# Channel shuffle on one core: the small first tiles replaced by full ones

## The chip, the cores and the metric

The kernel runs on one core of one Trainium2 chip. The time is the device time of one execution in microseconds (us); less is better. Engines named here: VectorE (DVE in the profile) copies within the on-chip memory SBUF, SyncE (SP) and ScalarE (ACT) issue transfers here and do nothing else, and 16 DMA engines move the bytes between HBM and SBUF.

## The reference

```
x: (16, 64, 64, 256) float32, groups = 8
x = x.reshape(batch, h, w, groups, 32)
x = x.transpose(0, 1, 2, 4, 3)
out = x.reshape(batch, h, w, 256)
```

Each of the 65,536 pixels has 256 channels, 1 KB. Within a pixel the channels are read as 8 groups of 32 and written as 32 sets of 8: out[j*8 + g] = x[g*32 + j]. No arithmetic is done. The kernel must read 67.1 MB and write 67.1 MB.

## The kernel before

The input is seen as one flat run of pixels. A piece of q slots is 128 x q pixels: partition p of SBUF holds q consecutive pixels, q KB, so each partition row of a transfer is one contiguous run of q KB in HBM and in SBUF. `_SLOTS` says how the 512 slots are cut: a list of tiles, each a list of its pieces. The first tile has two pieces, of 4 and 8 slots; the second has one of 28; then come twelve tiles of 38 and one of 16.

Every tile takes a load buffer and a store buffer of 38 KB a partition (`biggest`), from a pool of two (`_IN_BUFS`) and of three (`_OUT_BUFS`), in turn. The loop over the tiles (line 45) does for each one:

- line 55: SP issues the load of each piece. It must wait until the copy that last read this load buffer, two tiles back, has ended.
- line 57: VectorE copies each piece from the load buffer to the store buffer and permutes the channels on the way. It waits for the piece's load, and for the store that last used this store buffer, three tiles back.
- line 61: ACT issues the store of each piece, after its copy.

The order on each engine is that of the program; nothing else schedules. So there are two DMA queues, SP's for all loads and ACT's for all stores, each in program order, and both run on the same 16 DMA engines. At the start the loads of the first two tiles are issued without a wait; every later load is issued at the end of a copy, together with a store.

Of the kernel before, what the change touches and what calls it, by code (L numbers as in the profile page):

```python
# [1 line left out]

# [4 lines left out]


F32 = mybir.dt.float32
P = 128  # L10

_SLOTS = [[4, 8], [28]] + [[38]] * 12 + [[16]]
_IN_BUFS = 2
_OUT_BUFS = 3


@with_exitstack
def kernel(
    ctx: ExitStack,
    tc: tile.TileContext,  # L20
    x: bass.AP,
    groups: bass.AP,
    out: bass.AP,
):
    nc = tc.nc
    b, h, w, c = x.shape
    G = int(groups)
    CPG = c // G
    assert G * CPG == c
    assert sum(map(sum, _SLOTS)) * P == b * h * w  # L30
    biggest = max(map(sum, _SLOTS))

    x_flat = x.rearrange("b h w c -> (b h w c)")
    out_flat = out.rearrange("b h w c -> (b h w c)")

    in_pool = ctx.enter_context(tc.tile_pool(name="in_pool", bufs=_IN_BUFS))
    out_pool = ctx.enter_context(tc.tile_pool(name="out_pool", bufs=_OUT_BUFS))

    def rows(flat, first, q):

        return flat[first * c : (first + P * q) * c].rearrange("(p f) -> p f", p=P)

    ctx.enter_context(tc.manual_schedule(engines=None))
    first = 0
    for parts in _SLOTS:
        in_tile = in_pool.tile([P, biggest * c], F32, name="in_tile")
        out_tile = out_pool.tile([P, biggest * c], F32, name="out_tile")
        at = 0
        pieces = []
        for q in parts:  # L50
            pieces.append((q, first, slice(at * c, (at + q) * c)))
            first += P * q
            at += q
        for q, start, cols in pieces:
            nc.sync.dma_start(out=in_tile[:, cols], in_=rows(x_flat, start, q))  # L55
        for q, start, cols in pieces:
            nc.vector.tensor_copy(  # L57
                out=out_tile[:, cols].rearrange("p (i j g) -> p i j g", j=CPG, g=G),
                in_=in_tile[:, cols].rearrange("p (i g j) -> p i j g", g=G, j=CPG),
            )  # L60
            nc.scalar.dma_start(
                out=rows(out_flat, start, q), in_=out_tile[:, cols]
            )


# [1 line left out]
_INS = ['x', 'groups']  # L67
_OUTS = [((16, 64, 64, 256), 'float32')]

_NUMBERS = {'groups': 8}  # L70


# [26 lines left out]
```

## Time and profile before

| | before |
|---|---|
| time, median of 3 runs | 316.04 us (316.04 to 316.05) |
| profiled execution, span | 314.4 us |
| time less the span of the profiled execution | 1.6 us |
| VectorE busy | 119.0 us, 16 copies |
| copy of 38 slots | 8.79 us, 12 times |
| copies of 4, 8, 28, 16 slots | 1.09, 2.02, 6.57, 3.87 us |
| bytes moved | 134.22 MB, 427 GB/s over the span |
| first load issued, first copy, first store issued | 0.73, 4.06, 5.19 us |
| last copy starts | 294.54 us |
| issue to landing, load and store of 38 slots (median) | 37.0 and 42.6 us |

The page of the profile shows one execution. Its slices are fortieths of the span, and a digit there is the busy share in tenths; the DMA row is the mean over the 16 DMA engines. Queue q1 holds the loads (SP), q10 the stores (ACT). The chain is the list of steps that ended last, followed back from the last instruction; the view of waits adds up who waited for whom. A window is a stretch of the span with the busy time of each engine and the rate of the transfers in it; DMA packets are counted where they start, so a window of few packets may show a share over 1.

The profiled execution itself is longer than its span by what lies before the first and after the last instruction, which the profile doesn't show; the difference to the median of the timed runs is in the table.

### The profile page before, as it was taken

Reading aid. Unit: us, or ns where it says so; the run is one execution under the profiler, and the core shown is the slowest. Engines: PE = TensorE matmul, PEld = TensorE weight load, DVE = VectorE, ACT = ScalarE, POOL = GpSimd, SP = SyncE. Lnnn points to the kernel's source line nnn. Section 1 sums busy time; section 2 is a strip of 40 time slices with the busy share of each in tenths; the row PEclk is TensorE's granted clock in tenths of the full one; section 3 lists DMA queues with packets and bytes.
Section 4 is the critical chain, followed back from the end, with each engine's and each line's share of the span. In section 5 each row is a group of like instructions: output and inputs, shape, how many; then the busy total and the mean of one; then the engine's idle time right before and its main releaser. Section 6 shows DMA issues by size and latency. Waiting matters only on the chain.

```text
span 314.4 us, 132 instructions
## 1 busy us (share of the span) xinstructions
DVE 119.0 (38%) x16; POOL 0.2 (0%) x4
## 2 busy tenths in 40 slices
DVE  2081907309109109019028028037046055065400
POOL 0000000000000000000000000000000000000000
DMA  7999999999999999999999999999999999999997
GB/s 317 405 441 416 435 416 483 401 465 406 450 421 446 426 436 436 401 470 396 475 396 475 396 470 401 470 401 470 401 450 421 446 426 436 436 417 450 429 421 321
DMA packets 4608, 134.22 MB, mean 427 GB/s; under 512 B 512, under 2 KB 512, under 8 KB 768
## 3 DMA queue, kind: packets, MB, share of 16 engines
q1 hardware_dynamic: 2304, 67.11, 49.8%
q10 hardware_dynamic: 2304, 67.11, 49.4%
HBM read 67.11 MB, written 67.11 MB: 427 GB/s over the span
## 4 chain that ended last, share of the span: by engine, by line
DMA 76%; DVE 19%; issue 0%; SPq 0%; DVEq 0%
DMA in_tile<-in_x_dram 76%; DVE out_tile L57 19%; SPq L55 0%; DVEq L57 0%
## 5 line engine op out<-in xcount | busy, mean ns | idle before, releaser
L57 DVE COPY out_tile<-in_tile 128x9728 f32<-128x9728 f32 (+4 forms) x16 | 119.0, 7440 | 179.4 <-DMA in_tile<-in_x_dram 179.4
L80 POOL MEMSET const-uint8-127<- 128x1 uint8 x1 | 0.1, 103 | 0.0
L80 POOL MEMSET const-bfloat16-1.0<- 128x1 bf16 x1 | 0.1, 102 | 0.0
L80 POOL MEMSET const-float32-1.0<- 128x1 f32 x1 | 0.1, 100 | 0.0
L80 POOL MEMSET const-float32-0.0<- 128x1 f32 x1 | 0.1, 99 | 0.2 <-issue 0.2
## 6 DMA issues: line engine op xcount, KB each, us to landing
in_tile<-in_x_dram SPq DMA_DIRECT2D x12, 4864.0 KB, 37.0
out_dram<-out_tile ACTq DMA_DIRECT2D x12, 4864.0 KB, 42.6
in_tile<-in_x_dram SPq DMA_DIRECT2D x1, 3584.0 KB, 14.7
out_dram<-out_tile ACTq DMA_DIRECT2D x1, 3584.0 KB, 30.9
in_tile<-in_x_dram SPq DMA_DIRECT2D x1, 2048.0 KB, 30.4
out_dram<-out_tile ACTq DMA_DIRECT2D x1, 2048.0 KB, 15.2
in_tile<-in_x_dram SPq DMA_DIRECT2D x1, 1024.0 KB, 5.4
out_dram<-out_tile ACTq DMA_DIRECT2D x1, 1024.0 KB, 25.0
```

Source lines behind the costliest of these rows:

```text
L57: nc.vector.tensor_copy(out=out_tile[:, cols].rearrange("p (i j g) -> p i j g", j=CPG, g=G), in_=in_tile[:, cols].rearrange("p (i g j) -> ...
L80: nc = _bacc.Bacc("TRN2", target_bir_lowering=False, num_devices=1)
```

## The change

The cut of the 512 slots is another one. The tile of 4 and 8 slots and the tile of 28 slots at the head are gone; there are thirteen tiles of 38 slots, and the last tile has 18 slots in place of 16. The buffers (38 KB a partition, two for loads, three for stores), the loop and the engines stay as they are. Of 16 loads, 16 copies and 16 stores, 14 of each remain.

```
-_SLOTS = [[4, 8], [28]] + [[38]] * 12 + [[16]]
+_SLOTS = [[38]] * 13 + [[18]]
 _IN_BUFS = 2
 _OUT_BUFS = 3
```

## The prediction

> **What bounds the kernel now.** I read the page first: busy time, the 40 slices, the queues and the chain.
>
> ```profile
> span 314.4 us, 132 instructions
> ...
> DVE 119.0 (38%) x16; POOL 0.2 (0%) x4
> ...
> DMA  7999999999999999999999999999999999999997
> ...
> q1 hardware_dynamic: 2304, 67.11, 49.8%
> q10 hardware_dynamic: 2304, 67.11, 49.4%
> ...
> DMA 76%; DVE 19%; issue 0%; SPq 0%; DVEq 0%
> ```
>
> The 16 DMA engines are busy for 49.8 + 49.4 = 99.2% of the span; every slice but the first and last shows 9. VectorE works 38%. The chain gives 19% to the copies, but a chain passes through whatever released the next step. While VectorE copies, the other queue and the next load keep the DMA engines running, so only a copy during which both queues are empty would cost time. The view of waits agrees: all of VectorE's waiting is for loads, none for a free store buffer.
>
> ```profile
> DVE out_tile L57 <- DMA in_tile<-in_x_dram: 179.4, 16, 14.3
> ```
>
> Then the windows (the head, from copy to copy, the end) show how fast the bytes move in each stage (columns: window, its length, VectorE busy, GpSimd busy, clock, DMA share, GB/s).
>
> ```profile
> 1.50:2.00 0.50, 0.00 (x0) 0.00 (x0) 1.00 0.74 90
> 2.00:2.50 0.50, 0.00 (x0) 0.00 (x0) 1.00 0.45 164
> 2.50:3.00 0.50, 0.00 (x0) 0.00 (x0) 1.00 1.02 418
> 71.31:278.19 206.88, 79.13 (x9) 0.00 (x0) 1.00 1.00 433
> 294.54:313.30 18.76, 3.87 (x1) 0.00 (x0) 1.00 0.95 410
> 313.30:314.40 1.10, 0.00 (x0) 0.00 (x0) 1.00 0.00 0
> ```
>
> From 71.31 to 278.19 lie nine periods, each one 4,980,736-byte load and one such store: 9 x 9.961 MB in 206.88 us is 433.4 GB/s, 22.99 us a period. All 134.22 MB at that rate take 309.7 us. The span has 4.7 us more: 1.75 us before the first bytes (nothing moves before 1.5; the first row is a ramp), 1.1 us after the last ones, and some 1.9 us of small losses in between. So nothing big is to be had from the order of work; the question is whether the change opens a hole in which the DMA engines are empty.
>
> Last, the DMA view in windows that hold one size of row. A transfer is 128 partition rows, 8 on each engine (the page's 4608 packets are 32 transfers of 128 rows and 16 end marks).
>
> ```profile
> DMA packets 80, 1.31 MB, mean 437 GB/s; under 512 B 0, under 2 KB 0, under 8 KB 0
> ...
> q10 hardware_dynamic: 80, 1.31, 101.8%
> ```
>
> ```profile
> DMA packets 88, 3.42 MB, mean 428 GB/s; under 512 B 0, under 2 KB 0, under 8 KB 0
> ...
> q10 hardware_dynamic: 88, 3.42, 98.9%
> ```
>
> The first is 309 to 312 us, 16 KB rows of the last store: 3 us x 16 x 1.018 / 80 = 0.611 us a row. The second is 298 to 306 us, 38 KB rows: 8 x 16 x 0.989 / 88 = 1.438 us. The line through both is 0.009 + 0.0376 us per KB; it gives 0.160 for 4 KB, 0.310 for 8, 1.062 for 28, 0.686 for 18. Loads fit it: 2.6 to 3.4 us (4 KB, 80 rows, 100.1%) gives 0.160, and 4 to 5.5 us (8 KB, 77 rows, 102.1%) gives 0.318, 2% above it.
>
> **The change, part by part.**
>
> *Rows and instructions.* Work per engine before: 2 x 8 x (0.160 + 0.310 + 1.062 + 0.611) = 34.3 us for the four odd sizes, and 24 x 8 x 1.438 = 276.1 for the 38 KB ones, 310.4 in all. After: 26 x 8 x 1.438 = 299.1, and 2 x 8 x 0.686 = 11.0, 310.1. **Saved: 0.3 us**, all of it fixed cost of rows that are no longer there. SP and ACT issue 14 DMAs each where they issued 16 (0.33 and 0.36 us each), and VectorE makes 13 copies of 8.79 and one of 18 slots: (8.791 - 3.873) / 22 = 0.2235 us a slot, so 3.873 + 2 x 0.2235 = 4.32; in sum 118.6 for 119.0. These lie under the DMA engines' work and count nothing.
>
> *The head.* Now only loads move until the first store at 5.19; after the change nothing but loads moves until the first 38 KB tile is copied. Step by step: issue at 0.73, first bytes 1.75, the ramp costs 0.45 (90 and 164 GB/s against 433 in the rows above, beyond the 1.75), then 8 x 1.438 = 11.5: the load ends at 13.7. Its copy starts 0.6 later (the 4 KB load now: 1.75 + 0.45 + 8 x 0.160 = 3.48, copy at 4.06), at 14.3, and ends at 23.1. Here ACT issues the first store and SP the third load, as the third load waits for that copy to free the first of the two load buffers. From an issue to its first bytes it took 1.02 us (0.73 to 1.75), so both queues have work at 24.1. The second load covers all this: it was issued right behind the first, and its rows last until 13.7 + 11.5 = 25.2. **The cover is 1.1 us; no hole, and the later first store costs nothing**, as a byte that is loaded early is a byte that need not be loaded later. That head has some 15 rows of loads alone on each engine, 21.6 us. By the rows above loads alone run between the line and 2% over it: 0 to 0.43 us, of which I take half, **0.2 us paid**.
>
> [...]
>
> *What goes with the old head.* The window from 30.18 to 71.31 us (copies 4 to 6, with 28 KB stores still draining) moves 17.50 MB in 41.13 us, which at 433.4 GB/s would take 40.38: 0.75 us are lost, and from 32 to 36 us the rate is 397 GB/s. Rows are counted where they start, and half a 38 KB row per engine is 0.7 us, so the true loss is between nothing and 0.75; I take the middle, 0.37, and that it doesn't come again, since after the change all rows there are alike. **0.37 us regained**; its bounds are 0 and 0.75.
>
> *The middle.* Both queues hold 38 KB rows, half the rate each, period 22.99 as now. A copy needs the store three tiles back: the fourth copy, about 72, needs the first store, which runs from 24 to 48. No wait is added on VectorE.
>
> *The tail.* At 24 us, 15 of 112 load rows per engine are done. The 89 left of 38 KB alternate with stores: 89 x 2 x 1.438 = 256, to 280; the 8 of 18 KB with 8 stores: 8 x (0.686 + 1.438) = 17, to 297. Left are 7 store rows of 38 KB (10.1 us, to 307.3) and 8 of 18 KB (5.5). The last copy must be stored before 307.3: its load lands by 299 (loads under store traffic reached VectorE about 2 us late), copy 4.3, issue 1.0: 304.4. Cover 2.9. The store before it is needed at 295 (seven pairs of 2.12 after 280) and there by 282 + 8.8 + 1.0 = 292. Cover 3. Now the last copy ends at 298.4 and the stores at 313.3, so neither tail shows.
>
> *Sum.* -0.3 + 0.2 - 0.37 = -0.46 us on a span of 314.4, to 313.9. The median stands 1.6 us over the span (316.04), and that part stays: **315.6 us**. With the terms at their bounds: from -0.3 - 0.75 = -1.05 to -0.3 + 0.43 = +0.13, 315.0 to 316.2.
>
> **The rivals.**
>
> *A hole at 25 us: slower.* Place: between the end of the second load's rows and the first bytes of the third load or first store. Against it: 1.02 us from issue to bytes at the start. For it: the store issued at 5.19 had no row under way by 9.0 (the window 4 to 9 us holds rows of the load queue alone), 3.8 us or more. There, though, load rows stood ahead, and nothing ran empty. Price: an issue that takes x us leaves x - 2.1 empty. It counts as slower when the hole eats the 0.46 and 0.63 more, at x = 3.2; at 3.9 the hole is 1.8 and the time 316.04 - 0.46 + 1.8 = 317.4. Chance 0.11.
>
> *Loads alone are slower than the mix.* For: 410 GB/s from 2.6 to 3.4, with loads only; against: 4 KB rows explain it, and the stores alone keep 1.438. If 410 held for 38 KB rows, 21.6 us become 22.8: 316.04 - 0.3 + 1.2 = 316.9, slower. Chance 0.08. [...]
>
> *The whole small loss was the mixed sizes' own.* Then the sum is at its low end, 315.0.
>
> **How the numbers follow.** A measurement of this kernel can tell about 0.2%, 0.63 us, from no change: under 315.41 is faster, over 316.67 slower. Engines full throughout: 0.76; of its range 315.0 to 316.2 about two fifths lie under 315.41: 0.30 faster, 0.46 the same. The hole: 0.08 slower, 0.03 too small to tell. Loads alone slower: 0.06 and 0.02. What I don't see: 0.05, slower. The range is 315.0 to 316.7: the first case, and the small ends of the others.
>
> **What would show it.** Right: first copy near 14.3, first store and third load issued near 23.1, DMA share 9 in the slices around 25 us, periods of 22.99, no wait of VectorE for a store, and last bytes near 312.8. Wrong: a dip in a window of 24 to 28 us (the hole), under 425 GB/s from 3 to 23 us (loads alone), or longer periods. The last could come from loads and stores that now change over within a row or two of each other, where they were several us apart; the change between two stores alone, near 308, shows no dip in the slices, so I put nothing there.

## The result, and the profile after

| | before | after |
|---|---|---|
| time, median of 4 runs each | 316.05 us | 332.5 us (332.08 to 332.61) |
| ratio | | 1.0515, 95% interval 1.0502 to 1.0528 |
| span of the profiled execution | 314.4 us | 330.8 us |
| VectorE busy | 119.0 us | 118.7 us |

The kernel is 5% slower, 16.4 us; 315.6 was forecast. The page of the kernel after shows nothing of it at first sight:

```profile
span 330.8 us, 121 instructions
...
DVE 118.7 (36%) x14; POOL 0.2 (0%) x4
...
DMA  8999999999999999999999999999999999999994
...
q10 hardware_dynamic: 2016, 67.11, 50.5%
q1 hardware_dynamic: 2016, 67.11, 47.7%
```

The DMA engines are as busy as before (98.2% for 99.2%), VectorE still waits for loads alone, and its waits are longer, 198.6 us in all for 179.4:

```profile
DVE out_tile L57 <- DMA in_tile<-in_x_dram: 198.6, 14, 17.6
```

So the engines are not idle; the same bytes keep them busy for longer. One thing stands out: the two queues moved the same bytes, but the stores (q10) took 50.5% of a longer span and the loads 47.7%, where they were nearly equal (49.4 and 49.8%). The DMA view of the window from 100 to 200 us, in the middle of the steady part, makes it a time per row (a line of a queue has its packets, MB, and the time of its packets as a share of 16 engines' window):

```profile
DMA packets 1191, 41.21 MB, mean 412 GB/s; under 512 B 132, under 2 KB 132, under 8 KB 132
...
q10 hardware_dynamic: 596, 20.62, 52.4%
q1 hardware_dynamic: 595, 20.58, 47.6%
```

The same window of the kernel before:

```profile
DMA packets 1247, 43.54 MB, mean 435 GB/s; under 512 B 128, under 2 KB 128, under 8 KB 128
...
q10 hardware_dynamic: 624, 21.79, 50.4%
q1 hardware_dynamic: 623, 21.75, 50.3%
```

16 engines have 1600 us in the window. After: 20.62 MB are 530 store rows of 38,912 bytes, 1600 x 0.524 / 530 = 1.582 us each, and the loads 1600 x 0.476 / 529 = 1.440. Before both are 1.440. So **a store row takes 10% longer, a load row not**. The windows put the rest of the loss in its place:

```profile
24.00:26.00 2.00, 0.00 (x0) 0.00 (x0) 1.00 1.24 389
26.00:28.00 2.00, 1.30 (x1) 0.00 (x0) 1.00 0.81 195
28.00:30.00 2.00, 2.00 (x1) 0.00 (x0) 1.00 0.96 389
30.00:32.00 2.00, 2.00 (x1) 0.00 (x0) 1.00 0.81 350
71.00:296.00 225.00, 79.10 (x9) 0.00 (x0) 1.00 1.00 412
```

From 24 to 32 us 331 GB/s on average, 1.9 us behind 433. From 71 to 296 us it is 412 GB/s for 433. The third and the thirteenth copy in the timeline:

```profile
53.00 8.97 DVE L57 COPY out_tile<-in_tile 128x9728 f32<-128x9728 f32 x1 [17.55 <-DMA in_tile<-in_x_dram]
296.08 8.77 DVE L57 COPY out_tile<-in_tile 128x9728 f32<-128x9728 f32 x1 [15.29 <-DMA in_tile<-in_x_dram]
```

These are 10 periods of 24.31 us for the 22.99 of before, 13.2 us lost. The store rows themselves are 8 x 0.142 = 1.14 us a period, 11.4 in ten. Most of the rest is in the first two periods, 24.68 and 25.09 us, in which the slowest engine falls behind the others; the eight after them average 24.16. The dip and the ten periods make 15.1 of the 16.4 us. The saving of 0.3 us has to be made good too; what is left, 1.6 us, is the ramp at the start, the stores that are slow before 53 us, and the engines' uneven end (197 GB/s from 323 to 330 us), less what the old head lost.

What sets the slow rows apart is seen in the trace's single DMA records. They don't name the engine, but a row starts within some 4 ns of the end of the one before it on its engine, so the rows can be put into 16 chains. In these, while both queues have work, load and store rows take strict turns on each engine (595 packets of loads and 596 of stores from 100 to 200 us); a turn is one row of 38 KB here, 1.44 us of a load and 1.58 of a store. A transfer is 8 rows and an end mark on each engine, nine turns, in both queues (2016 packets a queue are 14 transfers x 16 engines x 9), so the distance between them, once set, stays, as the table below shows. In the kernel after the end marks of a load and a store come on the same engine in the same moment, and store row r runs directly behind load row r. In the kernel before store row 0 runs behind load row 2. Start of the end marks in us, kernel after, from the records (first, median and last engine of each transfer):

```
third to sixth load    48.2  51.1  52.6 |  71.2  75.1  77.2 |  94.2  99.3 102.3 | 117.1 123.5 126.7
first to fourth store  50.6  51.1  52.6 |  74.1  75.1  77.2 |  97.0  99.3 102.3 | 120.1 123.5 126.7
```

Median and last are the same in both rows: 15 engines, more or less, in step. The first engine isn't: its stores end some 2.9 us, one row of each kind, behind its loads, its store rows take 1.44 us, and this engine alone keeps 23.0 us a period (48.2, 71.2, 94.2, 117.1). At 187.8 us it has run so far ahead that no row of the next load, issued at 184.2, has come. Load and store start together there, and from then on it takes 24 to 25 us like the others (end marks 211.8, 236.5, 260.6).

### The profile page after: what moved, and what is told of

The parts are those of the page before. It is cut to its first block, busy times and chain, and to the rows that moved or that the text cites. A ratio compares the mean times of both kernels' runs of the same rounds, so it can differ in the third digit from the quotient of the medians.

```text
span 330.8 us, 121 instructions
## 1 busy us (share of the span) xinstructions
DVE 118.7 (36%) x14; POOL 0.2 (0%) x4
## 2 busy tenths in 40 slices
DMA packets 4032, 134.22 MB, mean 406 GB/s; under 512 B 448, under 2 KB 448, under 8 KB 448
## 3 DMA queue, kind: packets, MB, share of 16 engines
q10 hardware_dynamic: 2016, 67.11, 50.5%
q1 hardware_dynamic: 2016, 67.11, 47.7%
## 4 chain that ended last, share of the span: by engine, by line
DMA 78%; DVE 17%; issue 0%; SPq 0%; DVEq 0%
DMA in_tile<-in_x_dram 78%; DVE out_tile L57 17%; SPq L55 0%; DVEq L57 0%
## 5 line engine op out<-in xcount | busy, mean ns | idle before, releaser
L57 DVE COPY out_tile<-in_tile 128x9728 f32<-128x9728 f32 (+1 forms) x14 | 118.7, 8477 | 198.6 <-DMA in_tile<-in_x_dram 198.6
```

The costliest lines, as they stand in the source:

```text
L57: nc.vector.tensor_copy(out=out_tile[:, cols].rearrange("p (i j g) -> p i j g", j=CPG, g=G), in_=in_tile[:, cols].rearrange("p (i g j) -> ...
```

## The experiments

**Turns.** Four theories: (1) a store row is slow when the row just before it on its engine is the load of the same number, into the same partition; (2) it is the coinciding end of two transfers; (3) the distance of the two rows in HBM; (4) all engines storing at once. The tool is a small extra load of 16 x n partitions into a scratch tile, which nobody reads: on one queue it takes n rows and an end mark on each engine, n + 1 turns (with 16 partitions the page of `first30_s2` below counts 16 rows and 16 end marks more than that of `first30`, 4064 packets for 4032). The ratios below are to the kernel before, with their 95% intervals.

`s_later2`: the kernel after, with

```
             nc.scalar.dma_start(out=rows(out_flat, start, q), in_=out_tile[:, cols])
+            if first == 38 * P:
+                nc.scalar.dma_start(out=turn_tile[:16, :], in_=...)   # 16 rows of x
```

> The kernel after, with one 8 KB load of 16 partitions put on ACT's queue behind the first store: one row and one end mark for each DMA engine, so from there on each store row comes two turns later against the loads. Theory 1 (same partition): a store row is slow, 1.58 us for 1.44, when the row the engine moved just before it was the load into the same SBUF partition; two turns later it never is. Period back from 24.16 to 22.99 us, 11.6 us less of slow rows and some 2.5 less of uneven engines at the end: 318.5 us, 317.5 to 319.5. Theory 2 (load and store transfers change over at the same moment) and theory 3 (the two rows lie at a fixed distance in HBM) expect the same here. Theory 4 (all engines storing at the same moment are limited by the write side) expects no change: 332.5.

320.1 us (1.0127, 1.007 to 1.0183). The DMA view from 100 to 200 us:

```profile
q10 hardware_dynamic: 627, 21.64, 50.1%
q1 hardware_dynamic: 615, 21.44, 49.7%
```

1600 x 0.501 / 556 = 1.442 us a store row, and two extra turns in one place have taken 12.4 us off; the time is 0.6 us above the expected range. Theory 4 falls, since all engines still store at once. What is left, 4 us over the kernel before, is the hole at 25 us (78 GB/s from 26 to 28 us, 370 in the next two), the first store, which is slow until the shift takes hold, and an uneven end: 37 GB/s from 316 to 318 us.

`before_l3` and `before_l2`: the kernel before, the same load on SP's queue (32 and 16 partitions). It stands behind the load of the first 38-slot tile, at 8.9 us in the timeline; the expectations call that tile the second.

```
             nc.sync.dma_start(out=in_tile[:, cols], in_=rows(x_flat, start, q))
+            if first == 78 * P:
+                nc.sync.dma_start(out=turn_tile[:32, :], in_=...)     # before_l2: [:16]
```

> The kernel before, with one 16 KB load of 32 partitions put on SP's queue behind the load of the second 38-slot tile: two rows and one end mark for each engine, so the loads come three turns later against the stores. In the kernel before a store row follows the load row of three partitions further on; three turns later it follows the load into its own partition. Theories 1, 2 and 3: the stores turn slow, 1.58 us a row, periods of about 24.1 us, some 10 periods: 316.0 + 10 x 1.15 + 2 = 328 to 331 us. Theory 4: 316.1.

316.5 us (1.0008, 0.9997 to 1.0019): no change, and store rows of 1600 x 0.497 / 552 = 1.441 us. The same view, 100 to 200 us:

```profile
q1 hardware_dynamic: 624, 21.79, 50.4%
q10 hardware_dynamic: 616, 21.48, 49.7%
```

I had counted one turn too many: in the kernel before it is load row 2 that store row 0 runs behind, and the records give a row's place in its transfer, not its partition. In those of `before_l3` store row 0 runs directly *ahead* of load row 0, and the end marks of both queues coincide. So the miss is of use: theory 2 falls, since the ends coincide and nothing is slow.

> The kernel before, with one 8 KB load of 16 partitions on SP's queue behind the load of the second 38-slot tile: loads come two turns later, so store row r runs directly behind load row r on each engine, as in the kernel after. (In the kernel before store row 0 follows load row 2; with three turns it came just ahead of load row 0, and nothing was slow.) Theory 1 (a store row directly behind the load row of the same number, which lies in the same partition): stores turn slow from about 50 us on, 10 periods of 24.1 us for 23.0, 326 to 331 us. Were the slow stores of the kernel after due to its head (uneven engines, late first store): 316.3.

327.1 us (1.0348, 1.0318 to 1.0378). The same view, 100 to 200 us:

```profile
q10 hardware_dynamic: 600, 20.86, 53.1%
q1 hardware_dynamic: 592, 20.55, 47.5%
```

1600 x 0.531 / 536 = 1.585 us a store row, the loads 1.439. With its head, its sizes and its even engines untouched, the kernel before becomes slow by an 8 KB load that sets the turns as in the kernel after. That it is not the extra load as such, `before_l3` shows, which has a larger one.

The order doesn't act at once, though. In the records of the kernel after, rows 0 to 3 of the first store (28.0 to 39.3 us) run directly behind the load rows of the same number on 15 engines and take 1.44 us; rows 4 to 7 take 1.48, 1.54, 1.57 and 1.62. In `before_l2_half` below, the rows in this order take 1.44 us up to 60 us, and 1.69 on average from 64 to 80. On the other side, of the 38 KB store rows that run behind a load row of another number in the kernel before, `before_l3`, `s_later2` and `first12_s4`, over 5,500 in all, none takes over 1.5 us. So the order is needed, but it isn't the whole condition: something builds up first, and no run here shows what.

`read_next_row` and `read_mirrored`: the kernel after, reading elsewhere

```
+            off = 38 if q == 38 else 0                           # read_next_row
+            in_=rows(x_flat, start + off, q)
+            src = 12 * 38 * P - start if q == 38 else start      # read_mirrored
+            in_=rows(x_flat, src, q)
```

> The kernel after, but each 38-slot load reads HBM 38 pixels a partition further on (what the neighbour partition should get), so the output is shifted: the distance in HBM between a load row and the store row behind it changes by 38 KB, to that which the one fast engine has, while SBUF partitions, turns and queues stay. Theory 3 (distance in HBM): stores fast, 318.5 us. Theories 1, 2 and 4: 332 us, store rows 1.58 us.

> The kernel after, but the thirteen 38-slot loads read HBM in the reverse order of tiles (the output has the tiles in the wrong places): the distance in HBM between a load row and the store row behind it is another for every tile. Theory 1: as slow as the kernel after, every store row some 1.58 us, 330 to 333 us. Theory 3 (distance in HBM): most tiles fast, under 322 us, and rows that differ from tile to tile.

331.2 and 330.5 us, store rows 1.588 and 1.573, from the stores' lines of the two views of 100 to 200 us (528 and 543 rows):

```profile
q10 hardware_dynamic: 592, 20.55, 52.4%
q10 hardware_dynamic: 609, 21.13, 53.4%
```

At a distance of 38 KB more, and at another one for every tile, the rows are as slow: theory 3 falls as far as these distances go, all of them multiples of 38 KB. That the one fast engine has the first of these distances was my estimate, from its stores lying one row behind; the records have no addresses.

`pad`: `in_pool.tile([P, biggest * c + 176], F32, ...)` in the kernel after.

> The kernel after with 704 B of padding behind each load buffer, so that load and store buffers lie at another distance within a partition; turns, partitions and HBM as in the kernel after. Theory 1 in its plain form (same partition, whatever the address in it): 331 to 333 us, store rows 1.58 us. If it is the address within the partition that collides: 317 to 320.

329.6 us, store rows 1.556, which neither forecast had: with the buffers moved by 704 B within the partition the rows are 0.03 us shorter and the time 3 us, but it isn't cured. `warm` below is 3 us shorter as well, with the buffers where they were, so the 3 us can't be put down to the address.

**One engine or all.** `before_l2_one` and `before_l2_half`: `before_l2` with `turn_tile[:1, :]` and `turn_tile[:8, :]`.

> The kernel before, with a load of one partition (512 B) on SP's queue behind the load of the second 38-slot tile: it goes to one DMA engine alone, so that only this engine's loads come two turns later and its store row r falls directly behind load row r. Theory 1 in the form that the order on an engine itself makes its store rows slow: one engine at 24.1 us a period, the others at 22.99, and the one sets the pace: 323 to 329 us. Theory 5 (the slow rows need many engines that move the same row numbers at the same time): one engine alone keeps 1.44 us a row, 316 to 317.

> The same with 8 partitions, which go to eight of the 16 engines. Form 1: eight engines slow, eight fast, 325 to 329 us, mean of the store rows in the middle about 1.51. Theory 5: as eight engines do share the row numbers, something between, 318 to 324.

337.2 and 333.6 us (1.0666 and 1.0552), more than either theory had. One engine is enough, theory 5 falls, and it is worse than all 16: the timeline of `before_l2_one` shows the copies at the pace of that one engine.

```profile
51.01 8.77 DVE L64 COPY out_tile<-in_tile 128x9728 f32<-128x9728 f32 x1 [11.96 <-DMA in_tile<-in_x_dram]
77.41 8.77 DVE L64 COPY out_tile<-in_tile 128x9728 f32<-128x9728 f32 x1 [17.63 <-DMA in_tile<-in_x_dram]
104.42 8.84 DVE L64 COPY out_tile<-in_tile 128x9728 f32<-128x9728 f32 x1 [18.24 <-DMA in_tile<-in_x_dram]
130.56 8.81 DVE L64 COPY out_tile<-in_tile 128x9728 f32<-128x9728 f32 x1 [17.29 <-DMA in_tile<-in_x_dram]
```

26.5 us a period, 3.5 over 22.99 and so 0.44 us a store row: 1.88 us, against some 1.58 where all engines are in step. The records agree: 23 slow store rows from 51 to 131 us, 1.89 on average, and all others 1.44. The other 15 go on at their own speed until their loads depend on it; from 155 us on more of them run in the slow order too, and the period is 24.2 to 24.7 us. In `before_l2_half` rows in the slow order take 1.69 us from 64 to 80 us, while rows two turns off keep 1.44 in the same run.

**Other distances.** `offsets`: `before_l3` with three loads more, of 8, 4 and 2 partitions.

> The kernel before with four small loads on SP's queue behind the load of the second 38-slot tile: of 32 partitions (all 16 engines, three turns), of 8 (eight engines, two turns more), of 4 and of 2 (four and two engines, two more each). Store row 0 then falls behind load row -1, -3, -5 or -7 on different engines (counted round the nine turns of a transfer: 8 is the end mark, so -1 is the turn before row 0, and -5 is row 4 of the transfer before, -7 its row 2), and on none behind row 0. Theory 1 (only the row of the same number is slow): all engines keep 1.44 us a store row, 316.5 to 317.5 us. [...]

329.8 us, 12 us over the range of theory 1; the records show that the four distances are not the reason. From 40 to 80 us all 164 store rows of 38 KB have 1.439 us, most of them at the four distances. But the engines now end a transfer up to 11 us apart, the fifth copy waits 22.8 us for the last one, and engines that were ahead run dry. When the late copy ends, SP and ACT issue a load and a store together; 11 of the 16 engines then start both at row 0, in step. Their rows keep 1.44 us for some 10 us more and then turn slow: in the view of 130 to 200 us a store row takes 1.59 on average. So distances -1, -3, -5 and -7 aren't slow by themselves, as far as these 40 us show, and 11 engines, once the queues had run dry, fell into the slow order.

**Sizes.** `unequal`: `_SLOTS = [[40], [40], [34], [34]] * 3 + [[40], [28]]`.

> The kernel after with tiles of 40, 40, 34, 34 slots in turn, so that a store row of 40 KB always falls behind a load row of 34 KB or the other way round. In the kernel after store rows kept their 1.44 us where load rows had another size (18 KB rows of the last load). If equal sizes are needed: no slow stores, the hole at 25 us and uneven engines stay, 318 to 321 us. If the same partition in turn is enough: 328 to 334.

341.4 us (1.08): the miss shows that rows need not be equal. In its records store rows of 40 KB behind load rows of 34 KB take 1.74 us on average from 60 us on, where the line through the rows (0.009 + 0.0376 us per KB) has 1.51, and those of 34 KB behind 40 KB 1.36 for 1.29. The reverse hint in the kernel after, 38 KB store rows of 1.44 us beside the last load's 18 KB rows, stays unexplained; here too the store rows beside the last load (34 KB behind 28 KB) have their normal 1.29.

**Halves.** `halves`: the kernel after, each load and each store as two transfers of 64 partitions, in opposite order.

> The kernel after, but each load is two transfers, partitions 0 to 63 first, and each store two, partitions 64 to 127 first: changeovers still fall together, but a store row follows a load into a partition of the other half. Theory 1 and theory 3: no slow rows, 318 to 319.5 us. Theory 2 and theory 4: slow stores as in the kernel after, 331 to 334 us.

433.1 us, and it settles nothing here: the loads alone, at the start, already run at 191 GB/s.

```profile
3.00:13.00 10.00, 0.00 (x0) 0.00 (x0) 1.00 0.93 191
```

The DMA view of this window, then of the same one in the kernel after:

```profile
q1 hardware_dynamic: 49, 1.91, 92.8%
q1 hardware_dynamic: 108, 4.20, 97.2%
```

A load row of 38 KB took 160 x 0.928 / 49 = 3.03 us in this load of partitions 0 to 63, and 160 x 0.972 / 108 = 1.440 in one of all 128. No run here shows why.

**The head.** `first30`: `_SLOTS = [[30]] + [[38]] * 12 + [[26]]`; `first30_s2`: the same with the extra load behind the first store; `warm`: the kernel after with 16 partitions loaded on ACT's queue ahead of everything.

> The kernel after with a first tile of 30 slots in place of 38 and a last one of 26 in place of 18: the third load is issued some 3.5 us before the second one's rows are through, where in the kernel after it came about 1.5 us before, and its first rows took 3 us. If late issue made that hole, it is gone, 2 us. Whether store row r falls behind load row r again is not settled by this size: with the same turns as after 328 to 331 us, with others 316 to 317.5.

> The same with a first tile of 30 slots, and the 8 KB load on ACT's queue behind the first store, two turns. Theory 1, if the plain 30-slot kernel has the turns of after: no slow stores and no hole, 315.5 to 317 us. If the hole at 25 us isn't due to the late issue: 318 to 320.

> The kernel after with one 8 KB load of 16 partitions on ACT's queue at the very start, before anything else. The first store of both kernels moved its first row 3.9 to 4.0 us after its issue, where SP's first load took 1.0. If that is the first use of ACT's queue, the store now starts within 1.5 us of its issue at 24.0, the hole shrinks from 2 us to 1 or less, and the first store row meets the loads one or two turns earlier, so that store row r falls just ahead of load row r or two turns off, not behind it: 316.5 to 318.5. If the delay stays, the turns stay too: 332.

329.2, 336.1 and 329.5 us. In `first30` the third load is issued at 19.80 for 24.00, and the dip falls from 1.9 us to 1.1 (20 to 28 us, 375 GB/s for 331) or 1.3 (21 to 29 us, 360 GB/s). It doesn't vanish. The kernel fell into the slow turns. In `first30_s2` the shift was set without knowing where the engines of `first30` stood: in its records about half of the engines end loads and stores together after the shift, the others don't; the view of 100 to 200 us gives 1.51 us a store row, a mean of fast and slow engines. `warm` is 3 us shorter than the kernel after, but not for the reason hoped for: its first store row runs at 28.2 us, 4.4 us after the issue, so the delay isn't that of ACT's first use, and the turns stay slow (store rows of 1.58 us). The first store waited 3.9 us in the kernel before, with 28 KB load rows ahead, and 4.0 in the kernel after.

`first12`: `_SLOTS = [[12]] + [[38]] * 13 + [[6]]`; `first12_s4`: the same with 48 partitions on ACT's queue behind the second store.

> A first tile of 12 slots in one piece, thirteen of 38, a last one of 6. The third load is issued near 9.5 us, eight us before the second one's rows are through, so no hole; and the first big store starts near 29 us, five or so load rows into the third big load, so store row r follows load row r+5 or so and nothing is slow: 315.3 to 316.2, a little under the kernel before (two transfers fewer, 0.1 us, and a different head). If any start with few small tiles falls into the slow turns: 326 to 331.

> The kernel first12 (12, thirteen of 38, 6), which fell into the slow turns, with a load of 48 partitions on ACT's queue behind the second store: four turns later. Theory 1: no engine has store row r behind load row r after that, store rows 1.44 us, 316 to 317.5 us. Some engines of first12 are a turn or two apart; if one of them comes to the slow turns by the shift, 325 to 330.

329.1 us (1.0415, 1.04 to 1.0429) and 317.7 us (1.005, 1.0033 to 1.0067). I had placed the first big store five rows into a load; the records have it at 34.3 us, where the third big load starts (33.4), in step again. Four turns later it is cured, 11.4 us; view of `first12_s4`, 100 to 200 us, 1600 x 0.504 / 560 = 1.440 us a store row:

```profile
q10 hardware_dynamic: 624, 21.79, 50.4%
q1 hardware_dynamic: 616, 21.48, 49.7%
```

None of the versions beats the kernel before.

## Why the prediction was wrong

- **The middle** is the step that failed: "Both queues hold 38 KB rows, half the rate each, period 22.99 as now." The period is 24.31. The row's cost was taken from a trace in which load and store rows stood two turns apart, and held to be a property of the row. In these runs it depended on the order: 1.44 us at the distances shown above, 1.58 when store row r followed load row r and had done so for some 10 us or more. `before_l2` shows it in the kernel before, `s_later2` and `first12_s4` cure it. It is 11.4 of the 16.4 us by the row times alone, 13.2 with the engines that fall behind.
- The prediction saw the place and priced it at nothing: loads and stores that "change over within a row or two of each other". The change-over of two stores, from which it argued, says nothing of it, since no load runs there. My own timeline (third load's rows from 25.2, first store's from 24.1) had shown that both would start together; I read it as a question of a hole alone.
- **The cover of 1.1 us** failed too. The first load's copy started at 15.19 for 14.3, the issue was at 24.00 for 23.1, and the first store row at 28.0 for 24.1. The rival's place (chance 0.11) lost 1.9 us, price given 1.8, but that match is luck: the rival priced empty engines, and by the records the 16 engines are empty for only 0.5 us on average between 24 and 32 us. The rest is the third load's first rows, which came in time, from 25.4 us, and took 2.9 us on average for 1.44. Alone the dip would have meant about 317.5. The issue-to-bytes time of 1.02 us was that of the very first load; the window for a queue that joins another, 3.8 us or more, was in hand and taken as the far end.
- The ramp of 0.45 us was short: on each engine the very first row of 38 KB took 1.9 to 2.7 us for 1.44 (records; 3 to 13 us: 420 GB/s), so the first load ended up to 1.1 us later than the 13.7 of the sum.
- The rival of slow loads is summed without the 0.37 us regained: with it the time is 316.6, not 316.9, and so just under the 316.67 that counts as slower. It didn't come true.
- **Right**: after their first rows loads alone run at full rate (428 GB/s from 3 to 23 us, 447 from 15 to 23); the copies and issues lie under the DMA work; no wait for a store buffer; neither the last copy nor the number of instructions counts. The 0.3 us for rows can't be told from the rest.
- The range had only 0.05 for what I didn't see, and it was that.

Open: why the order costs time, and why only after a while. One engine alone paid (1.88 us a row); one fixed distance in HBM, one distance of the buffers and equal sizes were not needed (331.2 and 330.5, 329.6, 341.4 us). That the shared partition of theory 1 has a part in it isn't shown: the records have no addresses, it doesn't say why the first rows in the order are fast, and the same row number and the same partition were never parted, since the one try, `halves`, had load rows of 3.03 us from the start.

## What to carry to other kernels

This kernel, bound by two DMA queues, has a phase: which load row stands before which store row on each engine. It was set in the head, and kept while every transfer had 8 rows and an end mark on each engine and no engine ran dry (one did at 187.8 us in the kernel after, and its turns changed); the slow phase cost 3 to 7% with 38 KB rows, and in the kernel after the DMA engines' busy share was still 98.2% for 99.2%. For another kernel of this kind: compare time per row of both queues in a steady window, not the busy share; and shift one queue by a turn or two with a small extra transfer before rebuilding the head. What put them in step here was a load and a store issued at the same moment into queues that were dry or nearly so (the kernel after, `first12`, `offsets`).

## What the hardware showed that I had not expected

- A 38 KB store row took 1.44 us (kernel before, 100 to 200 us), or 1.58 directly behind the load row of the same number (kernel after, 100 to 200 us), or 1.88 where a single engine of the 16 had that order (`before_l2_one`, 51 to 131 us).
- The slow order needed time to act: 60 rows in it at 1.44 us first (kernel after, 28.0 to 39.3 us).
- A small load, placed once, moved the time by 11 to 12 us either way (8 KB: 316.1 to 327.1 and 332.5 to 320.1; 24 KB: 329.1 to 317.7).
- The first rows of a load that reaches a nearly dry queue took 1.7 to 3.5 us each, 2.9 on average, for 1.44 (records of the kernel after, starts from 25.4 to 28.2 us), most of the dip of 195 GB/s.
